# Ragged self-attention on one core: row masks fused into the normalizing products, zero fills queued behind the transposes, new orders for the narrow bodies and the prologue

## Chip, cores, metric

One Trainium2 chip (trn2), one core. The metric is the device time of one launch in microseconds (us), where lower is better. Two figures are in use: the time of a run, and the span in the trace, which runs from the first to the last instruction and is some 2 us shorter. With one core there is no second die to compare with, so each run is told with its **mean granted TensorE clock** (1.0 is full speed).

## The reference, cut to what matters

```python
x: (32, 512, 512) float32,  w_qkv: (512, 1536),  lengths: 32 integers from 64 to 511,  8 heads of 64
for b in range(32):
    n = lengths[b]
    q, k, v = split(x[b, :n] @ w_qkv)           # per head: (n, 64)
    p = softmax(q @ k.T / sqrt(64))
    output[b, :n] = p @ v                       # rows n..511 stay zero
```

## The kernel before: what the argument touches

The kernel sorts the sequences by length on the chip and runs two neighbours ("ranks" 2j and 2j+1) with one body of code that is compiled for a width of 32, 64, ... 512 columns; T is the number of 128-row tiles of that width. With this draw the bodies run in this order: 512, 448 (T = 4); 384, 352 three times, 320, 288 (T = 3); 256, 224 twice, 192, 160 twice (T = 2); 128, 96 (T = 1). A body has two halves, h = 0 and 1. A half does the attention of its own rank and, interleaved with it, the Q, K and V projections of the *next* rank. Between the last two-tile and the first one-tile body stands the *bridge*, a short piece that makes the first scores of the one-tile form. Evicting a bank means copying a result out of PSUM, the memory that the matmuls write, so that the bank is free for the next result. The order of the work is a string: S scores and exp, Q/K/B projections of queries and keys evicted by VectorE (small b: Q and K evicted by ScalarE), V the value projection, A attention times V with its normalization (R, M and X are its three steps where they are placed by hand), O and P the stores. In the profiles pa, psc and pav are the banks of projections, scores and attention, ep holds the exps, v_aug the V, onat the normalized output, zt the zeros.

```python
ORDER = {
    4: "S S Q0 A0 S S K0 V0 ... K3 V3 O",
    3: "S S Q0 A0 K0 S S V0 ... K3 V3 O",
    2: "S B0 S V0 A0 b1 A1 R1 M1 X1 V1 S S B2 V2 A2 A3 O V3 P B3",
}
# normalization of one pav bank: three VectorE instructions, two semaphore hops
recip: rcp  = 1 / den                                   # then s_r
mask:  rcp  = min(rcp, 3e38) * row_mask (0 or 1)        # waits s_r, then s_m
mult:  onat = num * rcp                                 # waits s_m

# one-tile half
qk(bank, Q);  qk(bank ^ 1, K)          # both evicted by VectorE
vproj(bank)                            # V of the next rank
attnv(h)                               # attention of this rank
scores(next rank);  act_store(h)       # exp, then the store, on ScalarE
```

The SyncE queue issues the transposes that make the next xT, the loads of x, and zero fills for the rows past each length. Fills are needed only in the first eight bodies: each covers its own ranks and two "mirrored" ranks far down the sorted order.

```python
def body(e, N):                        # SyncE
    if rank < 16:
        for h in range(2):
            zero_fill(mirrored rank, from tile 1)      # 768 KB, s_zm
            zero_fill(own rank, from tile T)           # s_zd
    for h in range(2):
        wait(s_xtf[h]);  to_xT(h, N)                   # transposes
        wait(s_xc[1 - h]);  load(1 - h, 5, T)
        ...
# ScalarE, at the head of the ninth body (rank 16): stores may not overtake fills
    e.wait_ge(s_zm, 16 * (B // 2))
# prologue (PE)
for i in range(4):
    qk(Q of i);  qk(K of i)
    if i == 0: acquire("a0"); acquire("a1")
    scores(i)                                          # right behind its own K
wait(V's weights);  vproj(0..3)
# SyncE / GpSimd: V's weights are loaded and cast before x of rank 1
```

## Time and profile before

| before | value |
|---|---|
| time given | 380.25 us median of 3 runs (379.88 to 382.26) |
| time in the runs beside the changed kernel | 381.23 us median of 4 |
| profiled span, clock | 376.5 us, 0.995 |
| TensorE / weight loads / VectorE / ScalarE busy | 92 / 64 / 65 / 59 % |

The prediction shows the main lines. One more view is of use, the waits of TensorE, summed by what it was about to write and who released it (us in total, times, longest):

```profile
PE pa L220 <- PEq L45: 9.3, 8, 2.3
PE pa L220 <- DVE v_aug L325: 4.1, 12, 0.7
PE pa L220 <- DVE qkT L292: 1.8, 4, 1.2
```

PEq L45 is the program's own helper that waits for a semaphore on TensorE's queue, so the first row doesn't name who released it; by its place in the program it is mostly the wait for xT, that is for the transposes. The second is V's bank, which VectorE empties too late. The third is a bank of Q and K. Most of these 15.2 us are what the change is after.

### The profile page before, as it was taken

What the parts mean: (1) busy time and instruction counts of PE and PEld (TensorE: products, weight loads), DVE (VectorE), ACT (ScalarE), POOL (GpSimd) and SP (SyncE); (2) the same over time, 40 slices, a digit from 0 to 9 for tenths busy, and PEclk for the clock granted to TensorE, in tenths of its full rate; (3) what the DMA queues carried; (4) which work ended last, traced back from release to release, by engine and by line L of the source; (5) the groups of instructions that cost most, each with busy time, mean ns of one, the idle gap of its engine ahead of it and who ended that gap; (6) DMA issues with size and microseconds to landing.
All of it is one profiled execution on the core that took longest, in us unless ns stands there. A gap on an engine that the chain in (4) does not pass through costs nothing. (4 is left out here: it accounts for less than half of the span.)

```text
span 376.5 us, 12671 instructions
## 1 busy us (share of the span) xinstructions
PE 347.0 (92%) x4844; PEld 242.5 (64%) x4845; DVE 244.2 (65%) x529; ACT 221.6 (59%) x291; POOL 58.1 (15%) x85
## 2 busy tenths in 40 slices
PE   7699999999999999999999979979999999989781
PEld 3255566666666666667666656766888778777660
DVE  4565666666666766667676756657767766776673
ACT  5486777777766665657666645655556445434230
POOL 3242020202011011101101110110211121112020
PEclk9999999999999999999999999999999999999998
DMA  7958983786388779678589589687785555665453
GB/s 269 341 115 274 259 204 111 278 166 163 114 328 199 180 281 214 172 278 216 185 277 240 220 216 207 259 198 212 189 164 173 184 151 167 180 169 172 141 162 88
DMA packets 84581, 76.42 MB, mean 203 GB/s; under 512 B 42544, under 2 KB 63024, under 8 KB 84528
## 3 DMA queue, kind: packets, MB, share of 16 engines
q1 hardware_dynamic: 69376, 59.47, 59.3%
q10 hardware_dynamic: 15152, 16.26, 12.9%
q8 instruction: 32, 0.52, 0.6%
q14 instruction: 21, 0.17, 0.2%
HBM read 29.37 MB, written 36.70 MB: 175 GB/s over the span
## 5 line engine op out<-in xcount | busy, mean ns | idle before, releaser
L262 ACT ACTIVATE ep<-psc 128x704 f16<-128x704 f32 (+5 forms) x265 | 204.1, 820 | 139.9 <-PE psc L220 89.5
L220 PE MATMUL pa<-xT,w_r 128*128 128x352 f16 (+11 forms) x1056 | 159.2, 286 | 13.2 <-PEq L45 8.2
L292 DVE CAST qkT<-pa 128x352 f16<-128x352 f32 (+5 forms) x180 | 101.2, 563 | 62.0 <-PE pa L220 59.9
L220 PEld LDWEIGHTS pa<-xT,w_r 128*128 128x128 f16 x1056 | 80.7, 98 | 64.6 <-issue 30.1
L220 PE MATMUL pa<-w_r,xT 128*128 128x128 f16 (+1 forms) x1296 | 94.7, 221 | 3.4 <-DVE qkT L292 1.2
L220 PEld LDWEIGHTS pa<-w_r,xT 128*128 128x128 f16 x1296 | 76.8, 98 | 21.3 <-issue 9.8
L325 DVE TENSOR_TENSOR v_aug<-pa,masks 128x384 f16<-128x384 f32 (+2 forms) x116 | 60.8, 524 | 28.6 <-PE pa L220 27.4
L220 PEld LDWEIGHTS pav<-v_aug,ep 128*128 128x128 f16 x1792 | 67.2, 98 | 9.5 <-issue 0.6
L220 PE MATMUL psc<-qkT 64*128 64x352 f16 (+11 forms) x656 | 69.9, 299 | 2.3 <-PEq L45 1.4
L220 PE MATMUL pav<-v_aug,ep 128*128 128x65 f16 x1792 | 71.7, 194 | 0.1
L418 DVE TENSOR_TENSOR onat<-pav,rcp 128x512 f32<-128x512 f32 (+1 forms) x68 | 53.4, 785 | 4.1
L866 POOL CAST v_aug<-masks 128x24 f16 (+4 forms) x33 | 9.1, 276 | 277.5 <-POOLq L677 277.5
L861 POOL CAST x<-x_nat 128x1536 f16<-128x1536 f32 (+3 forms) x34 | 44.0, 1293 | 18.6 <-POOLq L677 18.2
L220 PEld LDWEIGHTS psc<-qkT 64*128 64x128 f16 x656 | 20.6, 94 | 23.0 <-issue 12.5
L389 DVE RECIPROCAL rcp<-pav 128x8 f32<-128x8 f32 (+1 forms) x68 | 14.6, 215 | 15.6 <-PE pav L220 12.4
L396 DVE TENSOR_SCALAR rcp<-rcp,masks 128x4 f32<-128x4 f32 (+2 forms) x36 | 9.0, 249 | 3.5 <-DVEq L45 0.5
L900 PE MATMUL psc<-zt 128*128 128x512 f16 x26 | 7.3, 441 | 1.7 <-DVE zt L922 1.7
L405 DVE SCALAR_TENSOR_TENSOR rcp<-rcp,masks 128x8 f32<-128x8 f32 (+1 forms) x32 | 5.4, 170 | 4.2 <-DVE rcp L389 0.3
L290 ACT CAST qkT<-pa 128x448 f16<-128x448 f32 (+3 forms) x12 | 6.0, 499 | 3.3 <-ACTq L45 2.6
L631 ACT ACTIVATE ep<-tiny 128x1024 f32<-128x1024 f32 x6 | 6.0, 1051 | 0.0
L900 PEld LDWEIGHTS psc<-zt 128*128 128x128 f16 x26 | 2.7, 111 | 5.0 <-issue 1.7
L807 ACT CAST w_r<-w_f 128x1024 f16<-128x1024 f32 x4 | 4.2, 1046 | 1.2 <-DMA w_f<-in_w_qkv_dram 1.2
(49 smaller groups left out, 20.6 us busy)
## 6 DMA issues: line engine op xcount, KB each, us to landing
out_dram<-zt SPq DMA_DIRECT2D x16, 768.0 KB, 4.1
x_nat<-in_x_dram SPq DMA_DIRECT2D x12, 768.0 KB, 5.0
x_nat<-in_x_dram SPq DMA_DIRECT2D x8, 1024.0 KB, 5.4
out_dram<-onat ACTq DMA_DIRECT2D x28, 256.0 KB, 3.4
x_nat<-in_x_dram SPq DMA_DIRECT2D x12, 512.0 KB, 4.0
out_dram<-onat ACTq DMA_DIRECT2D x12, 384.0 KB, 2.9
out_dram<-onat SPq DMA_DIRECT2D x12, 384.0 KB, 4.6
out_dram<-zt SPq DMA_DIRECT2D x12, 256.0 KB, 4.0
```

The costliest lines, as they stand in the source:

```text
L220: return lambda e: e.matmul(o, lhsT, rhs, start=start, stop=stop)
L262: lambda e: e.activation(out=dst, in_=src, func=AF.Exp, scale=scale),
L290: group(pr, b, eng, mms, lambda e: e.copy(out=dst, in_=src))
L292: group(pr, b, eng, mms, lambda e: e.tensor_copy(out=dst, in_=src))
L325: lambda e: e.tensor_tensor(out=v_aug[h][:, 0:T, 2 * i : 2 * i + 2, 0:HD], in0=pa[:, bank, 0 : T * P].rearrange("p (t a d) -> p t a d", a= ...
L389: pr.add("dve", lambda e: e.reciprocal(out=rv, in_=den).then_inc(s_r, 1))
L396: lambda e: e.tensor_scalar(out=last, in0=last, scalar1=3.0e38, scalar2=now[0][:, 1, T - 1 : T], op0=ALU.min, op1=ALU.mult,).then_inc(s_m, 1),
L418: ins = e.tensor_tensor(out=dst, in0=num, in1=rv.unsqueeze(len(sh) + 1).broadcast_to([P, *sh, HD]), op=ALU.mult,)
L631: lambda e, i=i, a=a: e.activation(out=ep32[:, i + 1, a], func=AF.Copy, in_=tiny.unsqueeze(2).broadcast_to([P, NT, MAXS // 2]),).then_inc( ...
L861: e.tensor_copy(out=x16[h][:, 0:T, :], in_=x_nat[h][:, 0:T, :]).then_inc(s_xc[h], 1)
L866: e.tensor_copy(out=v_aug[h][:, 0:T, :, HD], in_=src[:, 0, 0:T].unsqueeze(2).broadcast_to([P, T, NH]),).then_inc(s_on[h], 1)
L900: e.matmul(psc[:, 1, 0, :], zt16[:, 0:P], zt16[:, 0:MAXS], start=True, stop=True)
```

## The change

Its intent: take one VectorE instruction and one hop out of each normalization, let the transposes go ahead of the fills, and give the short halves an order in which no eviction is waited for. Cut to its core:

```diff
-        def mask(): ...                    # 68 small operations and semaphore s_m
         def mult():
-            onat = num * rcp                                   # tensor_tensor over all tiles
+            full tiles (h == 0):  onat = num * rcp             # tensor_tensor
+            last tile, or each:   onat = (num * mask_t) * rcp  # scalar_tensor_tensor
-        2: "S B0 S V0 A0 b1 A1 R1 M1 X1 V1 S S B2 V2 A2 A3 O V3 P B3",
+        2: "S S V0 B0 A0 b1 A1 S V1 S B2 V2 O A2 A3 b3 P V3",
         if T == 1:
-            qk(.., K);  vproj(..);  attnv(..)
+            qk(.., K, "act");  attnv(..);  vproj(..)
         SyncE, body:
-            four fills at the head
             for h in range(2):
                 to_xT(h, N);  load(1 - h, 5, T)
+                fill own rank; fill mirrored rank     # if rank < 16
         prologue:
-            Q0 K0 [wait for both banks] S0  Q1 K1 S1 ...  V0 V1 V2 V3
+            Q0 K0 Q1 K1 S0  Q2 K2 S1  Q3 K3 S2  V0 S3 V1 V2 V3
-            load V's weights, then x of rank 1; cast in that order; loops begun before the casts
+            load x of rank 1, then V's weights; cast in that order; loops begun after the casts
```

More of the change, by code (lines that the diff above doesn't have):

```diff
@@ L167 @@
     s_r = sem("s_r")
-    s_m = sem("s_m")
     s_self = sem("s_self")
@@ L367, in attnv @@
             dst = dst.rearrange("p t (a d) -> p t a d", d=HD)
-            sh, cut, fin = [NT, 2], 2 * NT - 2, i % 2 == 1
+            sh, fin = [NT, 2], i % 2 == 1
         else:
-            n = 8 if T == 1 else 4 * T
-            res = pav[:, 0 : 74 * n].rearrange("p (j d) -> p j d", d=74)
+            sh, fin = [2, 4] if T == 1 else [T, 4], True
+            res = pav[:, 0 : 74 * sh[0] * 4].rearrange("p (b j d) -> p b j d", j=4, d=74)
             if T == 1:
-                res = res.rearrange("p (b j) d -> p b j d", b=2)
                 dst = on[:, :, 0, :].rearrange("p b (j d) -> p b j d", d=HD)
-                sh, cut = [2, 4], 0
             else:
-                dst = on[:, i // 2, 0:T, :].rearrange("p t (a d) -> p (t a) d", d=HD)
-                sh, cut = [n], n - 4
-            fin = True
-        n = sh[0] * sh[-1] if len(sh) > 1 else sh[0]
-        flat = rcp[:, i, 0:n]
-        last = flat[:, cut:n]
-        rv = flat.rearrange("p (j a) -> p j a", a=sh[1]) if len(sh) > 1 else flat
+                dst = on[:, i // 2, 0:T, :].rearrange("p t (a d) -> p t a d", d=HD)
+        rv = rcp[:, i, 0 : sh[0] * sh[1]].rearrange("p (j a) -> p j a", a=sh[1])
         num, den = res[..., 0:HD], res[..., HD]
@@ L389, in recip @@
             pr.add("dve", lambda e: e.reciprocal(out=rv, in_=den).then_inc(s_r, 1))
-        def mask():
-            pr.take("dve", s_r)
-            if h == 0 or T == 1:
-                pr.add(
-                    "dve",
-                    lambda e: e.tensor_scalar(
-                        out=last, in0=last, scalar1=3.0e38,
-                        scalar2=now[0][:, 1, T - 1 : T], op0=ALU.min, op1=ALU.mult,
-                    ).then_inc(s_m, 1),
-                )
-            else:
-                byt = flat.rearrange("p (t a) -> p t a", t=T)
-                pr.add(
-                    "dve",
-                    lambda e: e.scalar_tensor_tensor(
-                        out=byt, in0=byt, scalar=3.0e38,
-                        in1=now[0][:, 1, 0:T].unsqueeze(2).broadcast_to(list(byt.shape)),
-                        op0=ALU.min, op1=ALU.mult,
-                    ).then_inc(s_m, 1),
-                )
         def mult():
@@ L414, in mult @@
                 pr.take("dve", s_od[h][j], 16)
-            pr.take("dve", s_m)
-            def fn(e):
-                ins = e.tensor_tensor(
-                    out=dst,
-                    in0=num,
-                    in1=rv.unsqueeze(len(sh) + 1).broadcast_to([P, *sh, HD]),
-                    op=ALU.mult,
-                )
+            pr.take("dve", s_r)
+            if T == 1:
+                cuts = [(slice(0, 2), 0)]
+            elif h == 0:
+                cuts = [(slice(0, T - 1), None), (slice(T - 1, T), T - 1)]
+            else:
+                cuts = [(slice(t, t + 1), t) for t in range(T)]
+            def fn(e):
+                for w, t in cuts:
+                    ops = dict(
+                        out=dst[:, w], in0=num[:, w],
+                        in1=rv[:, w].unsqueeze(3).broadcast_to(list(num[:, w].shape)),
+                    )
+                    if t is None:
+                        ins = e.tensor_tensor(op=ALU.mult, **ops)
+                    else:
+                        ins = e.scalar_tensor_tensor(
+                            scalar=now[0][:, 1, t : t + 1], op0=ALU.mult, op1=ALU.mult, **ops
+                        )
                 if fin:
@@ L427, in mult @@
             pr.add("dve", fn)
-        todo = {"R": recip, "M": mask, "X": mult}
+        todo = {"R": recip, "X": mult}
         if not late:
@@ L483, in half @@
             qk(pr, st["bank"], g, [(i, 0) for i in range(NPAIR)], N, P)
-            qk(pr, st["bank"] ^ 1, g, [(i, 1) for i in range(NPAIR)], N, P)
-            vproj(pr, st["bank"], g, 0, 1)
+            qk(pr, st["bank"] ^ 1, g, [(i, 1) for i in range(NPAIR)], N, P, "act")
             read_class(pr, h, N)
-            pr.signals.append(s_xtf[g])
             pr.take("pe", s_on[h])
             attnv(pr, h, 0, 1)
+            vproj(pr, st["bank"], g, 0, 1)
             acquire(pr, f"a{st['bank'] ^ 1}")
+            pr.signals.append(s_xtf[g])
             scores(pr, h, g, 0, 0, 1, N)
@@ L510, in half @@
                 norm[i] = attnv(pr, h, i, T, f"X{i}" in toks)
-            elif k in "RMX":
+            elif k in "RX":
                 norm[i][k]()
@@ L618, in make_prologue, with unit @@
         bank = 0
-        for i in range(NPAIR):
-            for f in range(2):
-                qk(pr, bank, 0, [(i, f)], MAXS, MAXS)
-                bank ^= 1
-            if i == 0:
-                acquire(pr, "a0")
-                acquire(pr, "a1")
+        def unit(i):
             scores(pr, i % 2, 0, 0, i, 4, MAXS)
@@ L630, in make_prologue @@
                         "act",
-                        lambda e, i=i, a=a: e.activation(
+                        lambda e, a=a: e.activation(
                             out=ep32[:, i + 1, a], func=AF.Copy,
@@ L635, in make_prologue @@
                     )
+        for i in range(NPAIR):
+            for f in range(2):
+                qk(pr, bank, 0, [(i, f)], MAXS, MAXS)
+                bank ^= 1
+            if i > 0:
+                unit(i - 1)
         pr.add("pe", lambda e: e.wait_ge(s_wr["v"], 1))
@@ L639, in make_prologue @@
             bank ^= 1
+            if i == 0:
+                unit(3)
         return pr
@@ L714, in _ @@
             e.reg_mov(rank, 0)
-            mir = e.alloc_register("mirror")
             def to_xT(h, N):
@@ L741, in _ @@
                 ).then_inc(s_x0[t], 16)
-            e.wait_ge(s_x0[0], 16)
+            load(1, 1, NT)
             e.dma_start(
@@ L746, in _ @@
             ).then_inc(s_wv, 16)
-            load(1, 1, NT)
             for t in range(NT):
@@ L761, in body @@
                 next_class(e)
-                top = nc.cur_bb
-                lab, out_ = f"fill_b{N}", f"fill_x{N}"
-                e.br_lt(rank, B // 2, lab, out_)
-                nc.switch_bb(lab, parent=top)
-                for h in range(2):
-                    e.reg_add(mir, rank, h)
-                    e.reg_sub(mir, B - 1, mir)
-                    zero_fill(e, batch_of(e, mir, tmp, 0), 1, s_zm)
-                    if T < NT:
-                        zero_fill(e, batch_of(e, rank, tmp, h), T, s_zd)
-                    else:
-                        e.nop().then_inc(s_zd, 16)
-                nc.switch_bb(out_, parent=top)
                 for h in range(2):
@@ L780, in body @@
                     load(1 - h, 5, T)
+                    top = nc.cur_bb
+                    lab, out_ = f"fill_b{N}_{h}", f"fill_x{N}_{h}"
+                    e.br_lt(rank, B // 2, lab, out_)
+                    nc.switch_bb(lab, parent=top)
+                    if T < NT:
+                        zero_fill(e, batch_of(e, rank, tmp, 0), T, s_zd)
+                    else:
+                        e.nop().then_inc(s_zd, 16)
+                    e.reg_sub(tmp, B - 1, rank)
+                    zero_fill(e, batch_of(e, tmp, tmp, 0), 1, s_zm)
+                    nc.switch_bb(out_, parent=top)
                     if T > 1 and "P" not in ORDER[T]:
@@ L869, in ones @@
                 ).then_inc(s_on[h], 1)
+            cast(1, NT)
             e.wait_ge(s_wv, 16)
@@ L874, in _ @@
             ).then_inc(s_wr["v"], 1)
-            cast(1, NT)
             e.wait_ge(s_tab, 1)
@@ L966, in _ @@
             q.signal(s_tab)
-            begin_loops(e)
             for t in range(NT):
@@ L970, in _ @@
                 e.tensor_copy(out=x16[0][:, t, :], in_=x_nat[0][:, t, :]).then_inc(s_c0[t], 1)
+            begin_loops(e)
             rank_reg[0] = e.alloc_register("rank")
```

## The prediction

> **What bounds the kernel now.** I read the page first, then the waits, then the busy time by stage, and last the timeline around each stall of TensorE.
>
> The sorted draw of lengths makes 16 pairs, each run by one body with a first half (h = 0) and a second (h = 1): two bodies of four row tiles, six of three, six of two, two of one.
>
> ```profile
> PE 347.0 (92%) x4844; PEld 242.5 (64%) x4845; DVE 244.2 (65%) x529; ACT 221.6 (59%) x291; POOL 58.1 (15%) x85
> ```
>
> TensorE sets the time; VectorE and ScalarE matter only where TensorE waits for them. So the question is where TensorE stops. In the table of busy time by stage, the columns are stretch, length, and busy time of each engine:
>
> ```profile
> core 0: us, PE busy (x) PEld busy (x) DVE busy (x) ACT busy (x) POOL busy (x), PEclk, DMA share, GB/s
> 0.00:29.00 29.00, 21.90 (x152) 10.68 (x153) 14.69 (x37) 17.87 (x20) 9.64 (x22) 1.00 0.73 236
> ...
> 67.60:103.50 35.90, 35.90 (x506) 23.05 (x506) 23.91 (x49) 27.16 (x33) 4.39 (x4) 1.00 0.67 185
> ...
> 209.50:236.30 26.80, 24.30 (x354) 17.23 (x352) 16.72 (x36) 15.55 (x24) 3.52 (x4) 1.00 0.85 219
> ...
> 338.10:353.10 15.00, 12.75 (x220) 10.64 (x220) 10.40 (x27) 5.94 (x10) 2.34 (x3) 1.00 0.58 176
> ...
> 361.00:371.70 10.70, 6.45 (x113) 4.76 (x112) 7.95 (x16) 2.65 (x3) 1.66 (x4) 1.00 0.56 156
> ```
>
> The reader sees that the four-tile bodies (29 to 103.5 us) have no gap at all, and that idle time lies in the start, in some three-tile bodies, in the narrow two-tile bodies and in the one-tile tail.
>
> The three-tile gap, from the timelines of the SyncE queue and of TensorE in the fifth three-tile body (start, duration, what, idle before):
>
> ```profile
> 212.57 4.08 SPq L693 DMA_DIRECT2D out_dram<-zt  x4
> 216.78 4.81 SPq L721 DMA_TRANSPOSE xT<-x  x3
> ...
> 224.53 0.70 PE L220 MATMUL pa<-xT,w_r 128*128 128x320 f16 x4 [2.30 <-PEq L45]
> ```
>
> Four zero fills are issued ahead of the transposes that make the next xT, and TensorE then sits 2.30 us until xT is there. The same stands at 145.42 (0.80) and 250.67 (1.98): 5.08 us together.
>
> In the two-tile bodies TensorE waits for VectorE to empty V's PSUM bank:
>
> ```profile
> 341.44 0.23 DVE L396 TENSOR_SCALAR rcp<-rcp,masks 128x4 f32<-128x4 f32 x1
> 341.71 0.69 DVE L418 TENSOR_TENSOR onat<-pav,rcp 128x512 f32<-128x512 f32 x1
> 342.31 0.42 DVE L325 TENSOR_TENSOR v_aug<-pa,masks 128x256 f16<-128x256 f32 x1
> 342.78 0.45 PEld L220 LDWEIGHTS pa<-w_r,xT 128*128 128x128 f16 x8 [0.45 <-DVE v_aug L325]
> ```
>
> Weight loads of V for the next pair of heads start only when the eviction that stood behind mask and product is over. At the end of the run the tail is:
>
> ```profile
> 369.51 0.75 DVE L305 TENSOR_SCALAR v_aug<-pa,masks 128x512 f16<-128x512 f32 x1 [0.97 <-DVEq L45]
> 370.18 0.20 DVE L389 RECIPROCAL rcp<-pav 128x8 f32<-128x8 f32 x1
> 370.62 0.23 DVE L396 TENSOR_SCALAR rcp<-rcp,masks 128x8 f32<-128x8 f32 x1 [0.24 <-DVEq L45]
> 371.00 0.69 DVE L418 TENSOR_TENSOR onat<-pav,rcp 128x512 f32<-128x512 f32 x1
> ```
>
> The last reciprocal waits behind V's eviction, then comes the mask, then the product; the store after it (issued at 371.93) ends the span at 376.5.
>
> [...]in the narrow two-tile bodies TensorE reads 85% busy (12.75 of 15.00) but weight loads only 71% (10.64), and the weight-load rows show waits (0.45 above) of which the matmul row shows 0.25. I therefore sum those waits on the weight loads. [...]Here 512 elements took 691 ns and 768 took 957 ns[...]: an estimate of 424 ns for 256, 291 for 128, 557 for 384. [...] the last transpose of that group was issued by 221.6, and TensorE got xT at 224.5.
>
> **The change, part by part.**
>
> *Masks in the products.* 68 mask operations go (14.4 us busy, 9.0 + 5.4 in the groups), with one semaphore hop each. Products: four tiles, 8 of 384+128 and 8 of four times 128; three tiles, 12 of 512+256 and 12 of three times 256; two tiles, 24 of twice 256; one tile, 4 of 512. With the estimates: 8×0.848 + 8×1.164 + 12×1.115 + 12×1.272 + 24×0.848 + 4×0.691 = 67.9 us, against 53.4 + 14.4 = 67.8 now. Busy time doesn't change. But successive VectorE instructions overlap: mask start to product start is 0.27, product start to next start 0.60 (341.44, 341.71, 342.31), so a 256 would cost some 0.33. Reciprocal-to-free then shrinks by 0.27+0.60−0.66 = 0.2 us for two tiles, 0.2 for three tiles first half, under 0.1 for second halves. It pays only where TensorE waits for such a bank: in the three-tile bodies 18 weight-load waits on qkT, 6.9 us in sum[...]; I count 0.7 us saved. Four-tile bodies: nothing.
>
> *Zero rows behind the transposes.* In each half the transposes go first, then the load of x, then two fills. Transposes start 4.1 us earlier in first halves. At 320 columns xT would come at about 220.3 and is wanted at 222.2; at 288, 246.5 against 248.6. All three stalls go: **5.1 us**.
>
> *Start.* S of pair 0 no longer stops for both banks (0.88 us idle at 16.15), and x of rank 1 is loaded and cast before V's weights. The first body's wait for xT (1.77 us at 29.14) should go: x lands at about 16.0, the cast takes 1.90, four transposes 6.16, landing about 25.5. But ScalarE then paces it: the first exp comes at about 17.5 instead of 16.57, and its chain of four exps with six fills takes 9.4 us (16.57 to 26.0), so the last ends near 26.9 and the body's first projection starts near 27.4 instead of 29.14. Gain at most 1.7; I count **1.3**, as V's weights now arrive just when they are wanted (about 21.4 against 21.8).
>
> *Two-tile bodies.* One of two K/Q evictions per half leaves VectorE for ScalarE (12 × some 0.57 us), V3 is last, the mask is gone, and ScalarE issues the first store earlier, so it no longer holds up the next exps. The weight-load waits beyond the usual 0.16 to 0.21 us add up to some 5.9 us over the twelve halves, mostly at 160 and 192 columns. Laying out one 160-column half by hand: weight loads and switches 6.3 us, one remaining wait of 0.15 behind the first product, so about 6.45 against 7.4 now. At 256 columns 0.2 is won. Sum, 4×0.8 + 2×0.6 + 4×0.35 + 2×0.2 = 6.2; I count **4.5**.
>
> *Bridge and one-tile bodies.* The bridge waits 1.38 us for the last K/Q eviction behind a product; now only V3's is behind it: **0.7**. In the last two halves TensorE waits 1.17 and 1.15 us for K's eviction, because VectorE first does the earlier product; with K on ScalarE and attention ahead of V that goes (1.15 before the last half). In the last half attention starts right after K, about 1.8 us after its first weight load. The store however sits in ScalarE's queue behind the exp of the unused last S, which comes after V: about 2.25 us after attention ends, against 2.43 now. Attention ends near 366.4 instead of 369.5, so the store leaves near 368.65 instead of 371.93: **3.3**.
>
> Sum: 0.7 + 5.1 + 1.3 + 4.5 + 0.7 + 3.3 = 15.6 us. I take off some 1.6 for waits I can't see, so 14, which gives **366.2 us** from 380.25 (the profiled span 376.5 would go to about 362.5).
>
> **Rivals.**
>
> *ScalarE paces the short halves.* It gets evictions and both stores, in order, and a store waits for VectorE's product. For: one-tile bodies already show 15.8 us of ScalarE idle put down to its own queue; against: it is busy only 5.94 of 15.00 us at 160 columns. If so, half of the gain of two- and one-tile bodies goes: about 370.5.
>
> *The fills only move.* The 28 fills (16 of 768 KB, 12 of 256 KB)[...] now precede the next half's transposes. For: DMA share 0.74 to 0.92 in these bodies. Against: a half lasts 13 us, issue of two fills takes 2, and their 1 MB at some 230 GB/s 4.5, done before the next transposes. If so, 3 us come back: about 369.5.
>
> *The fused products are slow.* If scalar_tensor_tensor with PSUM input and a broadcast ran at half rate, VectorE would gain some 35 us of work and its evictions would stall three- and two-tile bodies: 380 to 390. Against: nothing but the small ones in the trace (128x8 in 0.17 us, fixed part only).
>
> **Range and chances.** The three-tile stalls and the tail are read directly from the trace and sum to 8.4; these alone give 371.9, just past 2% (372.6). The first two rivals together give some 374; the hand layouts in full give 364. So the range is 361.5 to 371.5. Faster by over 2%: 0.87; within: 0.11; slower: 0.02, the third rival.
>
> **What would show it.** TensorE's waits above 0.5 us on xT in the three-tile bodies absent; the first body's projection near 27.4; two-tile halves at 160 columns near 6.5 us; the stretch from the bridge to the last store near 15.0 instead of 18.7 us; the 128x256 products at 0.42 us, VectorE's busy time some 9 us lower and ScalarE's 8 higher. Wrong if new TensorE waits on ScalarE's evictions or on ep appear in the two-tile bodies, if xT is late in a different half, or if the fused products take more than 0.45 us.

## The result, and the profile after

**369.44 us** median of 4 runs (366.93 to 370.97) against 381.23 of the kernel before beside it (379.88 to 382.26): ratio 0.9686, interval 0.962 to 0.9753, 3.1% faster, some 11.8 us. Ratios here and below are the mean time of one kernel's fast runs over the mean of the other's fast runs of the same rounds, so they are not quite the ratio of the quoted medians. Executions over 1.5% slower than the fastest of the same kernel are left out of the means. All four runs are fast; their clocks are 0.986, 0.989, 0.998 and 0.986.

The page of the kernel after, busy time and the granted clock in 40 slices:

```profile
PE 349.1 (95%) x4844; PEld 245.4 (67%) x4845; DVE 236.9 (64%) x537; ACT 229.2 (62%) x307; POOL 58.0 (16%) x85
...
PEclk9699999999999999999999999999999999999998
```

VectorE is 7.3 us less busy, ScalarE 7.6 more; 9 and 8 were predicted. The clock row has a 6 in its second slice (9 to 18 us), which the profile of before does not have; more on it below. The waits of TensorE, in the same view as before:

```profile
PE pa L219 <- PEq L45: 2.6, 4, 1.2
PE pav L219 <- ACT ep L261: 2.4, 3, 1.1
```

Waits for xT fell from 9.3 to 2.6 us, V's bank no longer shows up, and the Q/K banks are down to 0.2 us. **A new row has come in**: attention waits three times for exp on ScalarE.

The fills, in the timeline of the SyncE queue after, at the same body whose 2.30 us stall the prediction shows:

```profile
212.23 3.81 SPq L707 DMA_TRANSPOSE xT<-x  x3
216.85 1.03 SPq L715 DMA_DIRECT2D x_nat<-in_x_dram  x1
218.58 1.59 SPq L681 DMA_DIRECT2D out_dram<-zt  x2
```

Transposes, then x, then two fills; the projection that follows (from 220.74) has no idle time before it.

The span by stage, from the starts of the first scores of each class in the timeline of TensorE (us, one profile each):

| stage | before | after | change |
|---|---|---|---|
| start to first scores of 448 | 67.6 | 69.2 | +1.6 |
| three-tile (384 to 256) | 157.9 | 152.3 | −5.6 |
| two-tile (256 to the bridge) | 91.3 | 87.8 | −3.5 |
| bridge to the last scores | 16.2 | 14.7 | −1.5 |
| last scores to the end | 7.1 | 7.3 | +0.2 |

The stretch left out, from the first scores of 448 to those of 384, takes 36.4 us in both. The sum is 8.8 us, the difference of the two spans (376.5 and 367.7), and less than the 11.8 of the medians. What the profiled pair lacks lies in the clock: 0.995 before, 0.986 after. The start is where it shows.

The timeline of TensorE and the busy time by stretch, after (columns as in the prediction: stretch, length, busy time of TensorE, weight loads, VectorE, ScalarE, GpSimd with counts, granted clock, DMA share, GB/s):

```profile
14.36 6.20 PE L219 MATMUL pa<-xT,w_r 128*128 128x512 f16 x16 [0.83 <-PEq L45]
...
10.00:14.30 4.30, 1.65 (x16) 1.04 (x16) 2.38 (x6) 1.17 (x2) 0.00 (x0) 0.82 0.91 292
14.30:20.40 6.10, 6.04 (x16) 2.10 (x16) 2.08 (x3) 0.00 (x0) 1.89 (x1) 0.56 1.00 378
```

The same stretch before:

```profile
14.30:20.40 6.10, 5.22 (x25) 1.86 (x23) 3.46 (x5) 3.83 (x5) 2.67 (x2) 1.00 0.97 355
```

After, 16 matmuls of 512 columns took 6.2 us at a clock of 0.56; before, 25 fitted into that stretch at 1.00. Was that the change's doing? That became the first question for the chip.

### The profile page after: what moved, and what is told of

It is laid out like the page before. It is cut to its first block, busy times and chain, and to the rows that moved or that the text cites.

```text
span 367.7 us, 12708 instructions
## 1 busy us (share of the span) xinstructions
PE 349.1 (95%) x4844; PEld 245.4 (67%) x4845; DVE 236.9 (64%) x537; ACT 229.2 (62%) x307; POOL 58.0 (16%) x85
## 5 line engine op out<-in xcount | busy, mean ns | idle before, releaser
L219 PE MATMUL pa<-xT,w_r 128*128 128x352 f16 (+11 forms) x1056 | 161.6, 288 | 3.8 <-PEq L45 2.6
L291 DVE CAST qkT<-pa 128x352 f16<-128x352 f32 (+5 forms) x164 | 92.0, 561 | 59.5 <-PE pa L219 55.5
L219 PEld LDWEIGHTS pa<-w_r,xT 128*128 128x128 f16 x1296 | 77.8, 98 | 18.4 <-issue 9.4
L405 DVE SCALAR_TENSOR_TENSOR onat<-pav,masks,rcp 128x256 f32<-128x256 f32 (+2 forms) x128 | 51.9, 444 | 5.2 <-DVE rcp L381 0.7
L844 POOL CAST x<-x_nat 128x1536 f16<-128x1536 f32 (+3 forms) x34 | 43.9, 1293 | 17.2 <-POOLq L665 16.2
L289 ACT CAST qkT<-pa 128x448 f16<-128x448 f32 (+3 forms) x28 | 14.1, 504 | 24.4 <-ACTq L45 15.2
L381 DVE RECIPROCAL rcp<-pav 128x8 f32<-128x8 f32 (+1 forms) x68 | 14.7, 216 | 19.7 <-PE pav L219 16.0
L403 DVE TENSOR_TENSOR onat<-pav,rcp 128x512 f32<-128x512 f32 (+2 forms) x32 | 17.8, 557 | 1.1
```

What stands on the lines that cost most here:

```text
L219: return lambda e: e.matmul(o, lhsT, rhs, start=start, stop=stop)
L289: group(pr, b, eng, mms, lambda e: e.copy(out=dst, in_=src))
L291: group(pr, b, eng, mms, lambda e: e.tensor_copy(out=dst, in_=src))
L381: pr.add("dve", lambda e: e.reciprocal(out=rv, in_=den).then_inc(s_r, 1))
L403: ins = e.tensor_tensor(op=ALU.mult, **ops)
L405: ins = e.scalar_tensor_tensor(scalar=now[0][:, 1, t : t + 1], op0=ALU.mult, op1=ALU.mult, **ops)
```

## Experiments

The theories:

- **My main theory**: the gain is the removed waits, term by term as predicted. Its rivals are the ones in the prediction.
- **Theory A** (the cold start): the clock fell because TensorE was nearly idle for a few us between 10 and 14 us, where only 16 transposes run, so filling that hole with dummy matmuls brings it back. **A1**: the changed load order (x of rank 1 ahead of V's weights) makes the hole. The rival to both: chance, in whatever kernel.

All kernels gave correct results. In the labels, a_ is the changed kernel with an edit, b_ the kernel before with an edit, w_ is a_warm with an edit, g_ is w_guard with an edit (g_tail starts from g_store). The kernel before had a median of 381.53 us (27 runs), 380.08 (11) and 381.63 (27). Each call ran on another chip, and the interval of a ratio is mostly some ±0.5%, or 2 us. So where kernels of two calls are compared, a difference of 1 to 3 us isn't settled by the run times: it rests on the profiles, one of each kernel.

### 1. a_warm: keep TensorE busy in the start

```diff
             for t in range(NT):
+                for _ in range((3, 0, 4, 0)[t]):
+                    e.matmul(psc[:, 1, 0, :], zt16[:, 0:P], zt16[:, 0:MAXS], start=True, stop=True)
                 e.wait_ge(s_c0[t], 1)
                 (four transposes of tile t)
+            for _ in range(3): (the same dummy matmul)
```

> The changed kernel with 10 dummy matmuls of 128x512 more: 3 ahead of the first transposes, 4 ahead of those of the third tile, 3 behind the last. Theory A (TensorE's granted clock fell because TensorE stood idle between its transposes, and the first projections paid half speed for it): the granted clock between 14 and 20 us is 1.0 instead of 0.56, the 16 first projections take 3.7 us instead of 6.1, and the whole kernel comes 2 to 3 us below the changed kernel's 369.4, near 366.5, with a mean clock of 0.995 or more. Rival B (the projections were slow because their operands or banks came late): clock and time don't move, 369.4.

367.49 us (365.69 to 368.6, 6 runs, clocks 0.991 to 0.999), ratio 0.9619 (0.9565 to 0.9674). The stretch from 14.3 us in a_warm:

```profile
14.30:20.40 6.10, 5.72 (x27) 2.13 (x26) 3.56 (x6) 1.62 (x2) 1.99 (x2) 1.00 1.02 386
```

The clock is 1.00 again: theory A holds, the hole is what costs the clock. From the first projection to the first scores of 448, a_warm takes 52.3 us against 54.8 in the changed kernel, so dummy work on an engine that waits anyway won 2.5 us there. That fits the changed kernel's own four runs: the one with a clock of 0.998 took 366.93 us, the other three 369.28 to 370.97. The run times of the two kernels alone would not prove it (intervals that overlap), and a_oldload and w_loads below, which differ in the dummies alone, have the same ratio (0.971 and 0.9716): there the start wins 1.5 us too (54.6 to 53.0), but the profile of w_loads loses as much in other waits. So that the clock would not blur the rest, most later kernels start from a_warm.

### 2. a_oldload: the old order of loads and casts, without dummies

```diff
-            load(1, 1, NT)
+            e.wait_ge(s_x0[0], 16)
             (V's weights)
+            load(1, 1, NT)
     (GpSimd: cast(1, NT) again behind the cast of V's weights)
```

> The changed kernel with the order of loads and casts of before: V's weights wait for the first x tile and go ahead of x of rank 1. Theory A1 (x of rank 1, issued without a wait, takes ring time from the third tile of the first x, whose cast came 1.08 us late; that gap is what lowered the clock): the third tile's cast again starts by about 11.1 us, the clock stays at 1.0, the first projections run in 3.7 us, but the first body then waits again for xT, 1 to 1.8 us near 29; the total near 367 to 368. Rival (the third tile is late for another reason, or the clock falls by chance from run to run): the time stays 369.4 with a mean clock near 0.987 in most runs.

369.84 us (369.24 to 373.15), ratio 0.971 (0.9651 to 0.9769), clocks 0.98 to 0.989. The stretch from 14.3 us still runs at 0.58. **A1 has fallen**: the hole isn't the new load order. b_masks and b_fills below settle it: there the prologue is the old one and the start is cold too (0.50 and 0.76 in the same stretch). The hole is in both kernels, and which run it chills differs from run to run (more on that under b_warm); the profile of before was a lucky one. Of 65 runs of the kernel before only 3 have a clock of 0.995 or more; their clocks range from 0.965 to 0.996, with a median of 0.981.

### 3. b_fills: the kernel before with only the fills moved

```diff
-                four fills at the head of the body
                 for h in range(2):
                     to_xT; load
+                    own fill, mirrored fill
```

> The kernel before with only the zero fills moved behind the transposes and the load. Theory (the fills held up the transposes): the three TensorE waits on xT in the three-tile bodies, 5.1 us, are gone and the time is 5 us lower, near 375.5 to 376.5. Rival (the fills only move and something else waits): less than 3 us, with a new wait in another half; ScalarE's guard on the mirrored fills before the first two-tile body, which took 3.3 us in the changed kernel, would be the place, worth about 1 us.

374.88 us (374.22 to 376.89, 4 runs, clocks 0.982 to 0.991), ratio 0.9841 (0.9769 to 0.9913), or about −6.0 us (the interval is 3.3 to 8.8, so the verdict at 2% is "unclear", but it is clear of no change). The three-tile stage takes 152.4 us instead of 157.9, and its waits for xT are gone. So this one move is about **half of the whole gain**. It also brings a wait of its own, 0.73 us for exp at 261.39.

### 4. b_masks: the kernel before with only the masks fused

```diff
-        mask(), s_m
+        scalar_tensor_tensor per masked tile, as in the change
-        2: "... A1 R1 M1 X1 V1 ..."
+        2: "... A1 R1 X1 V1 ..."
```

> The kernel before with only the masks moved into the products (the two-tile order is kept, its mask step left out). Prediction: VectorE's busy time stays at 244 us within 3, the time falls by 0.5 to 2 us (waits on VectorE in the three-tile and two-tile bodies a bit shorter). Rival (more and shorter products cost more than the masks saved): VectorE's busy time up by 5 us or more, and the time same or longer.

378.43 us (375.26 to 382.5, 22 runs; 378.07 over the 17 fast ones), ratio 0.9919 (0.9889 to 0.9949), about −3.1 us ("same" at 2%, but clear of no change), more than I expected. VectorE is busy 243.8 us, as expected, with 553 instructions instead of 529: the gain came with one semaphore hop less in each normalization and more instructions. The two-tile stage took 88.9 us instead of 91.3, and the stretch from the bridge to the end 22.3 instead of 23.3. This profile (span 379.3, clock 0.976) alone proves little; but the profile of w_order2, with the masks and the old order too, agrees (90.1 us, of which 1.07 is a wait at the guard that before doesn't have). The three-tile stage took longer here (160.4 instead of 157.9), with 6.7 us of waits for xT: the gain isn't made there. The fused product itself is *slower* than its tensor_tensor. From the groups by form of the kernel after:

```profile
L405 DVE SCALAR_TENSOR_TENSOR onat<-pav,masks,rcp 128x256 f32<-128x256 f32 x84 | 37.1, 478 | 3.5
L405 DVE SCALAR_TENSOR_TENSOR onat<-pav,masks,rcp 128x128 f32<-128x128 f32 x40 | 11.8, 344 | 0.8 <-DVE rcp L381 0.3
...
L403 DVE TENSOR_TENSOR onat<-pav,rcp 128x256 f32<-128x256 f32 x12 | 5.1, 424 | 0.4
```

478 ns against 424 at 256 elements: 54 ns more, and about as much more at 512 (751 against 691) and at 128 (344 against some 291, an estimate on the straight line through the measured 424 and 691). So by these sizes it is a fixed cost of 53 to 60 ns and no lower rate. Normalization is busy 69.7 us in sum (51.9 + 17.8) where the prediction said 67.9. It wins all the same. What has gone is one dependent step between reciprocal and free bank; that this step is the whole reason is argued, not tested.

### 5. w_order2: a_warm with the old two-tile order

```diff
-        2: "S S V0 B0 A0 b1 A1 S V1 S B2 V2 O A2 A3 b3 P V3",
+        2: "S B0 S V0 A0 b1 A1 R1 X1 V1 S S B2 V2 A2 A3 O V3 P B3",
```

> The changed kernel with the dummy matmuls of a_warm (so that the clock doesn't blur it), and the old order of the two-tile halves. Theory (part of the two-tile gain is the new order, with V3 last and one more eviction on ScalarE): the stretch from the first 256-column to the first 128-column scores, 88.5 us in a_warm of which 1.8 is the guard on the mirrored fills, becomes 2 to 3 us longer, and so does the time, 367.5 to about 370. Rival (the masks alone made the two-tile gain; b_masks alone brought 91.3 to 88.9): within 0.7 us.

369.56 us (368.6 to 370.31, 4 runs, clocks 0.993 to 0.996), ratio 0.9719 (0.9674 to 0.9764). The two-tile stage takes 90.1 us against 88.5 in a_warm. One wait differs between the two profiles and belongs to another part (see w_guard): the first attention of the 256 body waits 1.77 us for exp in a_warm and 1.07 here. Without that, the order is worth 1.6 + 0.7 = some 2.3 us by these two profiles.

### 6. w_tile1: a_warm with the old one-tile body

```diff
-            qk(.., K, "act");  attnv(..);  vproj(..)
+            qk(.., K);  vproj(..);  attnv(..)
```

> The same base with the old one-tile body (V ahead of attention, K evicted by VectorE). Prediction's claim: 3.3 us are lost again from the 128-column bridge to the last store. What the changed kernel's profile suggests instead: about 1.5 us, because the waits of 1.2 us on K's eviction were replaced by waits of 1.2 to 1.7 us on xT.

368.79 us (367.64 to 370.82, 4 runs, clocks 0.992 to 0.997), ratio 0.9701 (0.9649 to 0.9752). From the bridge's scores to the end of the span it takes 21.8 us against 21.3 in a_warm: 0.5 us by the profiles, 1.3 by the medians. (The difference of the ratios, 0.9701 against 0.9619, would be 3.1 us, but the intervals overlap.) I had predicted 3.3 for this part. The reason is in the comparison of the store's issue and landing:

| | bridge's scores to issue of the last store | issue to end of span |
|---|---|---|
| before | 18.7 | 4.6 |
| w_tile1 (old one-tile body) | 17.3 | 4.6 |
| after | 15.5 | 6.5 |
| a_warm | 15.7 | 5.7 |
| w_guard | 15.6 | 5.6 |

The last store *is* issued 3.2 us sooner after than before, nearly the predicted 3.7. But then it takes longer to land. The DMA view of the last 6.7 us of the kernel after (GB/s in 40 slices of 0.17 us, first the end of a load of x, then the store; the last line is that store, KB and us to landing):

```profile
GB/s 159 49 220 403 391 208 0 0 202 355 367 367 263 61 0 0 0 0 6 12 6 18 24 24 6 0 0 0 0 0 0 0 0 0 0 0 0 0 0 0
...
out_dram<-onat ACTq DMA_DIRECT2D x1, 256.0 KB, 4.4
```

The same of w_tile1, whose last 5.7 us these are:

```profile
GB/s 402 374 173 0 0 0 0 0 0 0 0 0 0 0 0 0 0 230 381 410 374 359 87 0 0 0 0 0 0 0 0 0 0 0 0 0 0 0 0 0
...
out_dram<-onat ACTq DMA_DIRECT2D x1, 256.0 KB, 2.4
```

In w_tile1 the store is one block of traffic and lands after 2.4 us. After, the block is followed by a pause and then by a trickle of 6 to 24 GB/s: 17 of the store's 272 packets, one DMA engine's share, move between 364.1 and 365.1, when all the others have ended by 363.3. In the trace's packet records an instruction fetch on the queue q8 takes from 362.4 to 364.1, and the trickle begins as it ends. Before and in w_tile1 the corresponding fetch was over 0.7 us or more before the store's first packet. So the sooner store met a **fetch of instructions** on one of its 16 DMA engines, and some 1.9 us of the 3.2 went there. (The records don't name the engine of a packet; that it is the same one is concluded from the times.) The other kept profiles bear it out. In the seven with the new one-tile order, apart from g_tail, such a fetch runs into the last store's packets: the store's last packet ends 1.0 to 1.1 us after the fetch does, and it lands after 2.9 to 4.4 us. In the six with V ahead of attention (before, b_fills, b_masks, b_warm, w_tile1, g_kact) the fetch is over before, and the store lands after 2.4 us each time. In g_tail the landing took 3.9 us with no such fetch: a load of x was still moving until 363.3, and may have delayed the store. In the page of before the queue q8, whose kind is instruction, moved 32 packets and 0.52 MB, that is 16 KB each; in the kernel after one of them, at the very end, went with a store that landed after 4.4 us instead of 2.4.

### 7. w_loads: a_warm with the old order of loads and casts

```diff
     (the edit of a_oldload, on a_warm)
```

> The same base with the old order of loads and casts (x of rank 1 behind V's weights). Prediction's claim: with a full clock the first body waits for xT again, so the first 448-column scores, at 67.0 in a_warm, come 1 us or more later. Rival (ScalarE's chain of exps paces the first body anyway, so the order of loads doesn't matter): they come within 0.4 us.

369.91 us (368.31 to 371.32, 4 runs, clocks 0.992 to 0.998), ratio 0.9716 (0.9668 to 0.9763). The first body's wait for xT is back, in part:

```profile
28.87 1.02 PE L219 MATMUL pa<-xT,w_r 128*128 128x512 f16 x4 [0.64 <-PEq L45]
```

From the first projection to the scores of 448 it takes 53.0 us against 52.3 in a_warm: the load order is worth 0.7 us. The rest of the 2.4 us between the two medians can't be laid to it: this profile shows a wait of 3.25 us for exp at the head of the 256 body (a_warm: 1.77) and one of 1.74 at the entry to the first three-tile body (a_warm: 0.90). That wait kept growing and shrinking from kernel to kernel, so it had to be looked at.

### 8. w_guard: a later place for ScalarE's guard

The new row of waits (2.4 us) has one large member. The timelines of TensorE and of ScalarE in the kernel after, at the ninth body (256 columns):

```profile
262.29 0.42 PE L219 MATMUL pav<-v_aug,ep 128*128 128x65 f16 x8 [1.06 <-ACT ep L261]
```

```profile
261.21 1.94 ACT L261 ACTIVATE ep<-psc 128x1024 f16<-128x1024 f32 x2 [3.28 <-DMA out_dram<-zt]
```

ScalarE stands at its guard until the last mirrored fill has *landed*, and with the fills moved to the end of each half the last one is on its way just then. The guard only has to precede the first store of that body, not its exps:

```diff
             def body(e, N):                     # ScalarE
-                if rank == 16: wait for all mirrored fills
+                if N > 256: the same guard at the head
         def act_store(pr, h, j, T):
+            if T < 3 and h == 0 and j == 0:
+                if rank of this body == 16: wait for all mirrored fills
```

> The same base, with ScalarE's guard on the mirrored zero fills moved, for bodies of one and two tiles, from the head of the body to just before its first store. Theory (the fills, moved later, land after the first two-tile body starts, so ScalarE's guard holds up its exps and TensorE waits 1.1 to 1.8 us for ep near 262): that wait is gone, the 256-column stretch falls from 17.9 to about 16.2 us, the time from 367.5 to about 366. Rival (the exps are late there for another reason, such as the jump between bodies): the wait stays.

364.92 us, the median of five fast runs from 364.29 to 366.27 (365.57 over all six), clocks 0.995 to 0.998, ratio 0.9601 (0.9562 to 0.9639): 4.0% below the kernel before and the **lowest ratio**, though g_kact and g_store below are within its noise. Against a_warm it is 2.6 us by the medians of fast runs and 0.7 by the ratios; the profiles show the mechanism. The wait is gone; the 256 body takes 15.9 us instead of 17.9 in a_warm, and the two-tile stage 86.0. One sixth run took 841.69 us at a clock of 1.0. I can't explain it. It did not recur in 14 runs of the three g_ kernels, which have the same guard.

### 9. b_warm: the dummies in the kernel before

```diff
     (the edit of a_warm, on the kernel before)
```

> The kernel before with the ten dummy matmuls of a_warm and nothing else. Theory (the cold clock at the first projections is a lottery of both kernels, which the profile of before happened to win): the mean clock is 0.99 or more in every run, and the time falls from about 381 to about 378.5. Rival (the cold clock belongs to the changed kernel): the time stays or rises by the dummy matmuls.

379.37 us (376.91 to 383.71, 20 runs), ratio of fast runs 0.998 (0.995 to 1.001). The median clock is 0.991 against 0.981, and the median of all runs is some 2 us lower, but the fast runs show no difference: the slow runs of before are the cold ones. So the expectation was met in part only. Its profile (381.8, 0.979; told for the clock alone) shows where the clock goes otherwise. The wait for xT in the timeline of TensorE, then the stretch before it and the one after it:

```profile
252.80 1.06 PE L220 MATMUL pa<-xT,w_r 128*128 128x288 f16 x4 [2.04 <-PEq L45]
```

```profile
250.00:252.80 2.80, 0.77 (x12) 0.38 (x10) 1.16 (x3) 1.45 (x3) 0.29 (x1) 1.00 0.71 199
252.80:257.00 4.20, 4.20 (x42) 2.80 (x43) 0.92 (x2) 0.79 (x2) 1.47 (x1) 0.59 0.91 240
```

After a wait of 2.04 us the clock is 0.59 for the next 4.2 us: the wait costs its length and then some 1.7 us more. The same followed a wait of 2.27 us at 30.4 (0.59) and one of 1.38 at 356.9 (0.72), but not one of 1.74 at 226.6, and in the profiled run of before it followed none (1.00 after the 2.30 us one). So the stalls that the change removed had cost *more in most runs than in the run that I predicted from*: with the start filled, b_warm's median clock is still 0.991, and only 3 of its 20 runs reach the 0.995 of that run. The length of a wait alone doesn't decide it: 2.04, 2.27 and 1.38 us were followed by a lower clock, 1.74 and 2.30 us were not.

The kept traces say more. In every one of the 14 the granted clock is 1.00 or 0.50 and changes only at multiples of 3.41 us (in the kernel after it is 1.00 for 6.83 us, 0.50 for 6.83 and 1.00 for 344.75, that is 2, 2 and 101 times 3.41), on a grid that lies differently in each run. (0.59 is an average over a stretch that ends later than the cold window.) Cut along that grid, TensorE's share of busy time in a window goes with the clock of the *next* one:

| run, window (us) | TensorE busy | clock in the next 3.41 us |
|---|---|---|
| b_warm 249.49 to 252.90, holds the wait of 2.04 | 0.40 | 0.50 |
| b_warm 222.18 to 225.60 and 225.60 to 229.01, share the wait of 1.74 | 0.79, 0.70 | 1.00 |
| before 222.87 to 226.28, most of the wait of 2.30 | 0.51 | 1.00 |
| start, before, 7.83 to 11.25 and 11.25 to 14.66 | 0.47, 0.68 | 1.00 |
| start, after, 9.37 to 12.79 | 0.41 | 0.50 |
| start, a_warm, the least busy one | 0.68 | 1.00 |

Of some 1460 full-speed windows in the 14 traces, all with a share of 0.45 or less were followed by 0.50 and all with 0.50 or more by 1.00; between them are three windows (0.46 and 0.47 kept the clock, 0.48 lost it). By these traces, whether a stall costs clock depends on how much of it falls into one window, which differs from run to run, and on how idle the rest of that window is. Of the experiments only a_warm, which took the start's least busy window from 0.41 to 0.68, tests it.

### 10. g_kact: V ahead of attention again, K still on ScalarE

```diff
             qk(.., K, "act")
+            vproj(..)
             attnv(..)
-            vproj(..)
```

> w_guard with V again ahead of attention in the one-tile bodies, K's eviction left on ScalarE. Theory (between the bridge and the last scores xT's round trip paces the halves, so the order of A and V matters only in the tail): the stretch from the first 128-column to the last 96-column scores stays within 0.5 us of w_guard's 14.7, the last product ends 0.7 to 0.9 us later, but the last store hardly moves because it waits for the exp anyway: the time within 0.5 us of w_guard's 365.6. Prediction's claim (attention ahead of V is worth a good part of 3.3 us): 1 us or more slower.

366.54 us (364.96 to 367.36, 4 runs), ratio 0.9618 (0.955 to 0.9686). From the bridge to the end it takes 22.6 us against 21.2 in w_guard, but by the time of the runs it is within the noise of w_guard and g_store. The last store is issued 18.1 us after the bridge instead of 15.6, and gets 1.1 of these 2.5 us back by landing sooner (4.5 to the end of the span instead of 5.6). Attention ahead of V is worth 1.4 us by the two profiles and 0 to 1 by the runs; more can't be said.

### 11. g_store: the one-tile store ahead of the exp

```diff
-            scores(..);  act_store(..)
+            act_store(..);  scores(..)
```

> w_guard with the one-tile bodies' store placed ahead of the exp on ScalarE's queue. Theory (the last store stands behind the exp of scores that nobody uses): the last store is issued some 0.7 us earlier, 365.6 to about 364.9. Rival (the store waits for the product, or the holding up of the exp costs as much in the halves before): no change.

365.9 us (365.32 to 366.53, 4 runs, clocks 0.995 to 0.999), ratio 0.9621 (0.9555 to 0.9687): no change against w_guard. The exp ahead of the last store cost nothing, because the store wasn't ready sooner: in both profiles it is issued 0.2 us after the product ends. And the exps, now behind the stores, made attention wait 0.54 to 0.59 us in three of the four one-tile halves, as the rival had it.

### 12. g_tail: attention at the head of the second one-tile halves

```diff
+            if h == 1: attnv(..); act_store(..)
             qk(.., Q);  qk(.., K, "act")
-            attnv(..)
+            if h == 0: attnv(..)
             vproj(..)
```

> g_store with attention at the head of each second one-tile half, ahead of Q and K. Theory (the end is attention, product and store of the last half; Q, K, V and scores of that half serve nobody, and the 1.0 us wait on xT stands ahead of attention): the last store leaves about 2.4 us earlier than in w_guard, while the second half of the first one-tile body may lose up to 1 us because attention waits for the exp there: 365.6 to about 364. Rival (attention at the head waits for the exp as long as Q and K took): no gain.

368.98 us (368.03 to 370.05, 6 runs, clocks 0.989 to 0.998), ratio 0.9696 (0.9645 to 0.9747): 3.1 us *slower* than g_store. My idea was to fill the wait for xT with the attention that is due anyway. The timelines of TensorE and ScalarE:

```profile
348.86 0.42 PE L219 MATMUL pav<-v_aug,ep 128*128 128x65 f16 x8 [2.44 <-PEq L45]
```

```profile
347.69 1.02 ACT L261 ACTIVATE ep<-psc 128x1024 f16<-128x1024 f32 x1 [2.09 <-ACTq L45]
```

Attention needs the exp of its own scores, issued directly before. That exp sits in ScalarE's queue behind the previous half's store, which waits for VectorE. So TensorE stands 2.44 us in one half and 2.17 in the other. The theory falls: one latency was traded for a longer one.

## Why the prediction was right, step by step

The forecast, 366.2 us in 361.5 to 371.5, held: 369.44 measured, 3.1% faster. Its sum was 14 us, the runs show about 11.8.

- **Three-tile stage: right.** Predicted 5.1 for xT and 0.7 for qkT (estimate), 5.8 in all; measured 5.6, and 5.5 from the fills alone (b_fills). So hardly anything of the 0.7 is seen. What the trace of before shows of the cause is the late issue, 4.08 us of fills ahead of the transposes; that the transposes also waited behind the fills once issued was not shown. The condition named in advance, no wait for xT above 0.5 us in these bodies, is met. By the runs' time the fills alone give about 6.0.
- **Start: right, hidden by the clock.** The prediction had the first body's projection at 27.4 instead of 29.14, that is 14.0 us after the first projection (13.39) instead of 15.75. In a_warm, at full clock, it is 28.58 − 14.70 = 13.9. In the kernel after it is 30.72, because its run was cold there; x also came 1 us later in that run. In a_warm TensorE has 0.40 us of idle time for the exp just before, so ScalarE paces it, as predicted. To the scores of 448, from the first projection on, a_warm wins 1.9 us (54.2 to 52.3); some 0.7 of it is the order of loads (w_loads); the rest was not split further. Predicted: 1.3, at most 1.7. The changed kernel itself had none of this in its profiled run (54.8).
- **Two-tile bodies and bridge: right but for a wait not seen.** Predicted 4.5 + 0.7 = 5.2, measured 3.5; in w_guard, without the guard's wait, 91.3 − 86.0 = 5.3. The masks give 2.4 of it and the order some 2.3. The prediction's first warning sign, new waits on exp, came true: 1.06 us at the guard, 0.46 and 0.90 in the first halves of the two 160-column bodies. Its second rival ("the fills only move") was the nearest to this: they did not hit a transpose, they hit whoever waits for their landing. The 160-column halves take some 6.9 us (27.58 for four) instead of 7.6, not quite the 6.5 of the hand layout.
- **One-tile bodies: mis-sized.** The term "3.3" measured 1.3 (the last two rows of the stage table; from the bridge on, the masks alone gave 1.0 in the profile of b_masks). The stretch from the bridge to the issue of the last store went from 18.7 to 15.5 (predicted 15.0), so that step is nearly right. What failed is the unspoken assumption that a store takes equally long to land: it took 4.4 us instead of 2.4. The prediction also misread the waits of 1.17 and 1.15 us in the last two halves: V goes into the bank that Q has filled, and in the profile of before V starts at 364.04 as Q's eviction ends (363.99), while K's runs on to 364.45. TensorE waited for Q's eviction, not K's, so moving K to ScalarE doesn't by itself free that bank. And the wait wasn't simply removed; the lines of TensorE in the last halves, before and then after, show what took its place:

```profile
364.04 1.04 PE L220 MATMUL pa<-w_r,xT 128*128 128x512 f16 x4 [1.17 <-DVE qkT L292]
```

```profile
357.82 1.52 PE L219 MATMUL pa<-xT,w_r 128*128 128x96 f16 x32 [1.17 <-PEq L45]
```

  The half got so short that the round trip of xT (release, transposes, landing) is what it now waits for.
- **Fused products: the criterion failed, the conclusion stood.** That a fused product takes as long as a tensor_tensor was my assumption, without a measurement; the times that I had estimated for tensor_tensor itself (a straight line through the measured 691 ns at 512 elements and 957 at 768 gives them within 1 ns) came out at 424 ns for 256 elements and 557 for 384 in the kernel after. 478 ns is over the 0.45 us that I had called wrong. The threshold was a bad one: with the extra 54 ns b_masks still gained 3.1 us. VectorE's saving came to 7.3 instead of 9 us.
- **Not foreseen: the clock.** The profile that I worked from had the clock at 0.995, where most runs of that kernel have about 0.981. The start's hole is still there after, and cost 2.5 us in a run that it chilled (54.8 us against 52.3 in a_warm).

The measured terms in sum, with the start taken from a_warm: 5.6 + 1.9 + 3.5 + 1.3 = 12.3 us at a full clock, against 11.8 by the medians. That the two are so close is partly luck: the runs behind the medians had other clocks. The 1.6 us taken off for waits not seen brought the forecast nearer; that they would be the landing and the guard was not foreseen.

**Open**: whether the share of busy time in a window is really what sets the clock, which no experiment tested on purpose; the varying wait, up to 1.7 us, at the entry to the first three-tile body, released by nothing that the profile shows (in the seven profiles where it is 0.6 us or more TensorE goes on 1.25 to 1.42 us after an instruction fetch on q8 ends, so it may wait for instructions; not tested); the varying landing time of the first x; the run of 841.69 us.

## What to carry to other kernels

When DMA work is moved out of the way of one waiter, look for everyone who waits for its *completion*: here a guard of one instruction, harmless at its old place, cost 0.7 to 3.3 us until it was moved to where it was needed. Read the granted clock of several runs before you size terms from one profile, because in b_warm a stall of TensorE of 2.04 us, which fell into one window of 3.41 us, was followed by 4.2 us at a clock of 0.59, which cost some 1.7 us more, and cheap dummy matmuls in a known hole are a fair test of that. And when a wait inside a short loop is removed, ask which latency comes next (the transposes' round trip, the exp behind a store, the landing of the last store), as it takes a share of the gain.
